# Full 128-row key and query blocks in the attentions of a two-layer encoder

## The chip, the cores and the metric

One core of one Trainium2 chip runs the whole program. The metric is device time in microseconds of one execution, as the median of several runs.

## The reference

Two pre-norm residual layers work on 1040 tokens: 16 learned meta tokens ahead of 1024 real ones, 1024 features wide, in float32.

```
layer 0:  oa = diff_attention(qa, ka, va)     4 heads, two softmaxes each, relative bias
          ob = gqa_dense(qb, kb, vb)          8 query heads on 2 key heads, normed and rotated
          h += concat(oa, ob) @ w_out
layer 1:  oc = window_gqa(qc, kc, vc)         16 query heads on 2 key heads, |i-j| <= 128,
          h += oc @ w_out                     the 16 meta keys always seen, a sink per head
both:     h += relu(norm(h) @ w_up)**2 @ w_down
out = norm(h)[16:]
```

In `diff_attention` the weights are `softmax(q0 k0) - lam * softmax(q1 k1)`, over all 1040 keys. In layer 1 only the 1024 real queries are needed, since the meta rows are dropped at the end.

## The kernel before, in words

Activations lie transposed, features on partitions and tokens along columns. A float32 product is done as several float32r passes over high and low parts (`kh`, `kl`, `vh`, `vl`, `ph`, `plo`), each part exact.

Tokens are cut in tiles of 128, with a ninth tile of 16: 1040 = 8 x 128 + 16. In layer 0 the tokens lie with the meta tokens first, so the ninth tile holds the last 16 tokens, as queries and as keys.

*Layer 0, projections.* `natural` (L292 to 300) transposes values to [token, feature], four tiles to a PSUM bank, the ninth as 16 rows; `store_v` and `load_v` pass them through DRAM, the ninth tile with a DMA of its own.

*Layer 0, attention.* `head_a` handles a differential head in four groups of query tiles, (0, 1), (2, 3), (6, 7, 8), (4, 5); `attend_b` handles two query tiles of a grouped-query head, 16 pairs for each key head, and one further group per key head with the 16 queries of the ninth tile of four heads side by side (64 rows). For a query tile `scores` makes q k in three chunks of 346 or 348 keys in PSUM, VectorE moves them to SBUF with the row minimum (L504, L507), and ScalarE takes the exponential (L516). A differential tile is then combined on POOL (L619, L620). The ninth query tile of a differential head has its two softmaxes in rows 0 to 15 and 32 to 47 of one 48-row tile; a matmul with `sel48` transposes and sums them (L545).

`pv` (L523 to 574) then multiplies with the values. The keys are taken in runs of two blocks for a 256-column group (one for the 272-column group (6, 7, 8)): transpositions to PSUM (`tr`, L543), a copy to `ph` on ScalarE (L557), the low part `plo` by a subtraction on VectorE (L559), and value matmuls to `pv` (L572). The ninth block is a run of its own:

```
kw = TW[runs[r][0]]
...
T.matmul(ps_o[:, :gw], vmats[v][:kw, j, :], (plo if lo else ph)[:kw, c],
         start=n_ == 0, stop=n_ == total - 1)
```

with `kw` = 16: two value matmuls over 16 rows for a grouped-query group (`passes` are (values, ph) and (values, plo)), three for a differential one (a third with the values' low part).

*Layer 1, attention.* For 8 pairs of heads and 8 query tiles (L1163 to 1248), scores cover two or three key blocks and the 16 meta keys, which lie between the blocks along the columns of the keys (400 or 272 columns). The values are multiplied by pairs of items; the meta keys are the last item, and their value matmuls go over `kw` = 16 rows (L1233). Their transposition takes 128 columns of the scores, and so brings 112 rows of other keys along; only in the last query tile (t = 7) the meta keys end the columns, and 16 are transposed.

*Order.* Code is written in dependency order, and a scheduler puts each engine's instructions in an order of its own ahead of time. Attention work is offered to it in pieces: `late` holds the value products of up to three groups (two in layer 1), whose pieces are run between scores. Each engine then runs its queue in order.

Of the kernel before, what the change touches and what calls it, by code (L numbers as in the profile page):

```python
# [74 lines left out]
def trunk(tc, hT, gT, w_in0, w_out0, w_up, w_down, w_in1, w_out1, rel, sinks, lamv, subln, qkn,  # L75
# [13 lines left out]
    def lay_out(pl, tags):  # L89
        """fix where a pool's slots lie: a first tile of each tag, in this order, handed to its first users."""  # L90
# [47 lines left out]
    def load_w(src, lo_on=V, parts=1, to=None):  # L138
        """a [128, 8 x 128] tile of weights as the split halves of its columns."""
# [6 lines left out]
    def mm3(ps, w, xh, xl, o, n, k0=0, k1=KT):  # L146
        """ps[:, :n] = the product over k from k0 to k1 (added to what is there if k0 > 0), columns o to o + n."""
# [6 lines left out]
    def rsqrt_small(x, pw, n):  # L154
        """1/sqrt(x) of a [pw, n] tile by three Newton steps from the shifted-exponent guess."""
# [27 lines left out]
    def colsum(acc, c0, n, ps, scale, eps=None):  # L183
        """rows of mean(acc over partitions)+eps, one column for each token tile, then 1/sqrt."""
# [20 lines left out]
    def bcast_cols(y, tiles, newps, use):  # L205
        """use(psum, first column, width) gets y's entries laid along the free axis on every partition."""
# [58 lines left out]
    def project0(m, scale=None, w=None, raw=False, tags=()):  # L265
        """[128 columns of the projection, tokens] of the normed input; raw: without the norm's factor yet."""
# [15 lines left out]
    def spill_pair(i, parts):  # L282
        """high and low parts of [128, tokens] to DRAM; parts: [(source, first column, width)]."""
# [18 lines left out]
    def store_v(dst, v):  # L302
        D.dma_start(dst[:, :8 * P], f32(v[:, :8]).rearrange("p a b -> p (a b)"))
        D.dma_start(dst[:16, 8 * P:], f32(v[:16, 8]))

    def load_v(v, src):
        D.dma_start(f32(v[:, :8]).rearrange("p a b -> p (a b)"), src[:, :8 * P])
        D.dma_start(f32(v[:16, 8]), src[:16, 8 * P:])

    # axial rotary tables times the norm's gain  # L310
# [17 lines left out]
    def rope(z, tab, fscale, i_out):  # L328
        """normalize and rotate a pair of heads [2 x 64, tokens]."""
# [58 lines left out]
    natural(zv, put_v)  # L388
# [3 lines left out]
    # relative-position bias vectors, negated, to DRAM  # L392
# [5 lines left out]
    # each copied to 128 rows: read back with a row pitch shorter by one, row p is shifted by p  # L398
# [19 lines left out]
    # lambda  # L418
# [10 lines left out]
    lam48 = cst.tile([48, 1], F32, name="lam48")  # L429
    V.memset(lam48, 1.0)  # L430
    V.tensor_copy(lam48[32:48], nlam[32:48])
    sel48 = cst.tile([48, 16], F32, name="sel48")
    V.memset(sel48, 0.0)
    for r in (0, 32):
        D.dma_start(sel48[r:r + 16], ident_d[0:16, 0:16])
# [7 lines left out]
    for h in range(4):  # L443
# [9 lines left out]
        natural(project0(8 + h), put)  # L453
        store_v(vA_d[h, 0], vh)
        store_v(vA_d[h, 1], vl)
# [236 lines left out]
    for g in range(2):  # L692
# [8 lines left out]
        for i in range(4):  # L701
            for t in range(0, 8, 2):
                if 4 * i + t // 2 == B_TAIL[g]:
                    attend_b(g, [(qt[:, :], 64)], store_t)
# [653 lines left out]
```

## Time and profile before

| | |
|---|---|
| median of 3 runs | 2626.34 us (2625.93 to 2629.81) |
| span of the profiled execution | 2630.9 us (the profile gives no further time of its own) |
| TensorE busy | 2508.9 us, 95% of the span |
| VectorE busy | 1937.8 us, 74% |
| ScalarE, POOL busy | 1265.7 and 1281.2 us |
| mean granted TensorE clock | 0.979 of full speed |
| layer 0 attention | about 269 to 727 us |
| layer 1 attention | about 1558 to 1842 us |

In a timeline each row is a run of like instructions: start, duration up to the end of the last, engine, line, operation, output and inputs, weights as rows x columns, the moving operand, and the count. `16*128` are weights of 16 rows and 128 columns. A matmul's printed duration holds its way through the array, so that successive ones overlap; the distance of starts tells what one takes of TensorE.

### The profile page before, as it was taken

What the parts mean: (1) busy time and instruction counts of PE and PEld (TensorE: products, weight loads), DVE (VectorE), ACT (ScalarE), POOL (GpSimd) and SP (SyncE); (2) the same over time, 40 slices, a digit from 0 to 9 for tenths busy, and PEclk for the clock granted to TensorE, in tenths of its full rate; (3) what the DMA queues carried; (4) which work ended last, traced back from release to release, by engine and by line L of the source; (5) the groups of instructions that cost most, each with busy time, mean ns of one, the idle gap of its engine ahead of it and who ended that gap; (6) DMA issues with size and microseconds to landing.
All of it is one profiled execution on the core that took longest, in us unless ns stands there. A gap on an engine that the chain in (4) does not pass through costs nothing. (4 is left out here: it accounts for less than half of the span.)

```text
span 2630.9 us, 42960 instructions
## 1 busy us (share of the span) xinstructions
PE 2508.9 (95%) x15440; PEld 2233.5 (85%) x15440; DVE 1937.8 (74%) x4057; ACT 1265.7 (48%) x2562; POOL 1281.2 (49%) x1214
## 2 busy tenths in 40 slices
PE   7999999999998999989999999999989999899997
PEld 7999888888898899988999988887868888676776
DVE  7834887798748566689898757777575656989975
ACT  3322656677634344453433547777344444443434
POOL 3300765333145223268877344556453223889854
PEclk9999999999998999999999999999989999999998
DMA  4378433200131532323232342232312332233322
GB/s 133 117 243 260 111 95 93 49 11 11 67 123 42 173 114 98 114 82 105 82 106 90 117 120 71 65 88 61 121 44 101 112 112 96 96 96 98 102 75 80
DMA packets 105494, 261.09 MB, mean 99 GB/s; under 512 B 16864, under 2 KB 48320, under 8 KB 104768
## 3 DMA queue, kind: packets, MB, share of 16 engines
q1 hardware_dynamic: 105280, 258.35, 30.9%
q8 instruction: 121, 1.98, 0.3%
q14 instruction: 93, 0.76, 0.1%
HBM read 191.40 MB, written 75.40 MB: 101 GB/s over the span
## 5 line engine op out<-in xcount | busy, mean ns | idle before, releaser
L854 PE MATMUL st<-h,wh 128*128 128x260 f32 (+1 forms) x2520 | 811.9, 326 | 45.3 <-DVE h L998 14.5
L854 PE MATMUL st<-l,wh 128*128 128x260 f32 (+1 forms) x2520 | 810.2, 324 | 6.6 <-DVE l L779 4.0
L854 PE MATMUL st<-h,wl 128*128 128x260 f32 (+1 forms) x2520 | 782.9, 325 | 14.8 <-DVE wl L135 8.8
L854 PEld LDWEIGHTS st<-h,wh 128*128 128x128 f32 x2520 | 480.3, 191 | 98.9 <-DVE h L998 19.9
L854 PEld LDWEIGHTS st<-h,wl 128*128 128x128 f32 x2520 | 474.4, 191 | 63.0 <-POOL wl L135 12.8
L854 PEld LDWEIGHTS st<-l,wh 128*128 128x128 f32 x2520 | 481.8, 191 | 45.0 <-DVE l L779 4.6
L134 ACT CAST wh<-wr 128x512 fp32r<-128x512 f32 x378 | 233.3, 619 | 408.7 <-PE st L854 228.7
L135 DVE TENSOR_TENSOR wl<-wr,wh 128x512 fp32r<-128x512 f32 x254 | 215.0, 848 | 178.9 <-ACT wh L134 178.3
L864 POOL TENSOR_TENSOR ws<-wr 128x512 f32<-128x512 f32 x32 | 43.2, 1350 | 412.7 <-DMA wr<-w_up 332.1
L135 POOL TENSOR_TENSOR wl<-wr,wh 128x512 fp32r<-128x512 f32 x124 | 177.0, 1430 | 67.0 <-ACT wh L134 62.2
L502 PE MATMUL sc<-stk,stk 128*128 128x346 f32 (+1 forms) x768 | 186.4, 356 | 8.1 <-DVE mx L504 7.9
L886 ACT ACTIVATE up<-up 128x260 f32<-128x260 f32 (+1 forms) x192 | 93.7, 491 | 193.2 <-DVE up L885 193.1
L516 ACT ACTIVATE sp<-sp,mn 128x1040 f32<-128x1040 f32 (+1 forms) x134 | 156.2, 1166 | 38.6 <-DVE mn L514 37.0
L998 DVE TENSOR_TENSOR h<-h,st 128x260 f32<-128x260 f32 x392 | 151.7, 417 | 29.7 <-PE st L854 27.3
L559 DVE TENSOR_TENSOR plo<-tr,ph 128x512 fp32r<-128x512 f32 (+3 forms) x260 | 153.4, 598 | 24.1 <-ACT ph L557 23.2
L557 ACT CAST ph<-tr 128x512 fp32r<-128x512 f32 (+3 forms) x260 | 130.3, 515 | 82.1 <-PE tr L543 56.5
L572 PE MATMUL pv<-ph,v 128*128 128x256 f32 (+3 forms) x594 | 157.3, 302 | 0.8 <-ACT ph L557 0.7
L998 DVE TENSOR_TENSOR hall<-hall,st 128x512 f32<-128x512 f32 x196 | 131.9, 681 | 31.2 <-PE st L854 28.7
L151 PE MATMUL mm<-l,wh 128*128 128x346 f32 (+3 forms) x440 | 150.9, 344 | 1.3 <-DVE l L762 1.2
L151 PE MATMUL mm<-h,wl 128*128 128x346 f32 (+3 forms) x440 | 150.1, 343 | 0.0
L151 PE MATMUL mm<-h,wh 128*128 128x346 f32 (+3 forms) x440 | 148.5, 344 | 1.2 <-ACT h L761 1.2
L673 POOL TENSOR_SCALAR sp<-sp,rsum 128x1040 f32<-128x1040 f32 (+1 forms) x66 | 74.2, 1138 | 152.5 <-DVE rsum L520 123.0
(273 smaller groups left out, 5943.0 us busy)
## 6 DMA issues: line engine op xcount, KB each, us to landing
wr<-w_down SPq DMA_DIRECT2D x68, 512.0 KB, 3.6
wr<-w_up SPq DMA_DIRECT2D x64, 512.0 KB, 3.5
stk<-stk_d SPq DMA_DIRECT2D x72, 260.0 KB, 7.0
sd<-up SPq DMA_DIRECT2D x28, 520.0 KB, 3.1
s<-sd SPq DMA_DIRECT2D x28, 520.0 KB, 3.1
sd<-up SPq DMA_DIRECT2D x28, 512.0 KB, 2.6
s<-sd SPq DMA_DIRECT2D x28, 512.0 KB, 3.5
wr<-w_in SPq DMA_DIRECT2D x27, 512.0 KB, 3.8
```

The lines of the kernel that those rows point to most:

```text
L134: A.copy(h, src)
L135: lo_on.tensor_tensor(l, src, f32(h), op=ALU.subtract)
L151: T.matmul(ps[:, :n], a[:, k % 4 * P:(k % 4 + 1) * P], x[k][:, o:o + n], start=(k == 0 and i == 0), stop=(k == len(xh) - 1 and i == 2))
L502: T.matmul(ps[:M, :n], q, k[:, o:o + n], start=(i == 0), stop=(i == len(ops) - 1))
L516: A.activation(s[:M, :L], s[:M, :L], AF.Exp, bias=mn[:M, x:x + 1], scale=-1.0, accum_out=sums[:M, x:x + 1])
L557: A.copy(ph[:kw, :w], pt[:kw, :w])
L559: V.tensor_tensor(plo[:kw, :w], pt[:kw, :w], f32(ph[:kw, :w]), op=ALU.subtract)
L572: T.matmul(ps_o[:, :gw], vmats[v][:kw, j, :], (plo if lo else ph)[:kw, c], start=n_ == 0, stop=n_ == total - 1)
L673: G.tensor_scalar(s[:M], s[:M], rs[:M, i:i + 1], 1.0, op0=ALU.mult, op1=ALU.mult)
L854: T.matmul(acc_[x, o][:, :n], a[:, c], b[:, o:o + n], start=first and k == 0 and y == 0, stop=k == nk - 1 and y == 2, skip_group_check=not ...
L886: A.activation(r[:, c], r[:, c], AF.Square)
L998: marks[0].append(V.tensor_tensor(ht[m][:, c], ht[m][:, c], acc_[x, o][:, :n], op=ALU.add).ins)
```

## The change

All value and selector matmuls of both attentions come to use 128 rows.

*Layer 0 keys.* `pv` takes eight whole blocks. For the last 16 keys it transposes the last 128 columns (keys 912 to 1039) and copies rows 96 to 127, whose lower half are the 16 keys, once for each pass into rows 0 to 31, 32 to 63 and 64 to 95 of a `tail` tile that was zeroed at the start; the low part is subtracted in place. One matmul multiplies it with a block of values that stacks the same tail: `natural_tail` writes the 16 value columns into columns 16 to 31 of each 32 of a padded tile (`vtail`), transposes that, and the third copy becomes the low part. So the two or three 16-row matmuls of a group become one.

*Layer 0 queries.* `qt` of a differential head and its selector are 128 wide, and the meta group of a grouped-query head is 128 wide (64 of them zero).

*Layer 1.* The value blocks become ten: eight of keys, one with the 16 meta values in rows 0 to 15 and zeros below, one with them in rows 112 to 127 and zeros above (for t = 7, where the last 128 columns are transposed). The meta item's copies and matmuls go over 128 rows; their number is as before.

The value tile is stored and loaded with one DMA; 646 instructions stand in the queue of SP in place of 663.

```diff
-    def natural(z, use):
-        for b in range(0, NT, 4):
-            n = min(4, NT - b)
+    vtail = pP.tile([P, 4, 32], F32, tag="vtail", bufs=1, name="vtail")
+    G.memset(vtail, 0.0)
+    def natural_tail(z, n, use):
+        A.copy(vtail[:, 0:n, 16:32], z[:, S:L].unsqueeze(1).to_broadcast([P, n, 16]))
+        pt = bank("nat")
+        T.transpose(pt[:, 0:P], vtail.rearrange("p a b -> p (a b)"), ident)
+        use(pt, 8, 1, P)
+    def natural(z, use, nt=NT):
+        for b in range(0, nt, 4):
+            n = min(4, nt - b)
...
-        natural(project0(8 + h), put)
+        def put_tail(pt, b, n, w):
+            A.copy(vh[:, 8], pt[:, :P])
+            V.tensor_tensor(vh[64:96, 8], pt[64:96, :P], f32(vh[64:96, 8]), op=ALU.subtract)
+        zv = project0(8 + h)
+        natural(zv, put, 8)
+        natural_tail(zv, 3, put_tail)
...
+    tails = [pA.tile([P, 272], F32R, tag="tail", bufs=3, name=nm("tail")) for _ in range(3)]
+    for t in tails:
+        G.memset(f32(t), 0.0)
...
-                    T.matmul(ps_o[:, :gw], vmats[v][:kw, j, :], (plo if lo else ph)[:kw, c],
-                             start=n_ == 0, stop=n_ == total - 1)
+                    T.matmul(ps_o[:, :gw], vmats[v][:, j, :], (plo if lo else ph)[:, c],
+                             start=n_ == 0, stop=False)
                     n_ += 1
+        yield
+        pt, _ = transposed([L - P])
+        tl = tails[tail_at[0] % 3]
+        tail_at[0] += 1
+        for x, (v, lo) in enumerate(passes):
+            rows = slice(32 * x, 32 * x + 32)
+            if lo:
+                V.tensor_tensor(tl[rows, :gw], pt[96:128, :gw], f32(tl[0:32, :gw]), op=ALU.subtract)
+            else:
+                A.copy(tl[rows, :gw], pt[96:128, :gw])
+        T.matmul(ps_o[:, :gw], vmats[0][:, 8, :], tl[:, :gw], start=False, stop=True)
...
-        qt = pA.tile([P, 2, 48], F32R, tag="qt", name=nm("qt"))
+        qt = pA.tile([P, 2, P], F32R, tag="qt", name=nm("qt"))
...
-        qt = pA.tile([P, 64], F32R, tag="qtb", bufs=2, name=nm("qt"))
+        qt = pA.tile([P, P], F32R, tag="qtb", bufs=2, name=nm("qt"))
+        G.memset(f32(qt[:, 64:P]), 0.0)
...
-                items = [(b, o, P) for b, o in blocks] + [(8, mo, NM)]
+                items = blocks + ((8, mo) if t < 7 else (9, wd - P),)
...
-                            T.matmul(po[:, :256], vp[g][:kw, b, :], pp[:kw, 256 * x:256 * x + 256], start=first,
+                            T.matmul(po[:, :256], vp[g][:, b, :], pp[:, 256 * x:256 * x + 256], start=first,
                                      stop=last and y == 1)
```

The scheduler's order moves with it. On TensorE, in the middle of the grouped-query heads, before: the ninth block of one group (`pv_6159`) stands as two value matmuls on `ph_6215` and `plo_6217`, six rows apart, with scores (`sc`) and the next group's first value matmul (`pv_6265`) between them.

```order
L502 MATMUL sc_6441<-stk_5187,stk_5212 128x348 [waits DVE_49]
L502 MATMUL sc_6441<-stk_5193,stk_5212 128x348
L572 MATMUL pv_6159<-ph_6215,v_5199 128x256 [waits Activation_49]
L502 MATMUL sc_6445<-stk_5187,stk_5212 128x346 [waits DVE_49]
L502 MATMUL sc_6445<-stk_5193,stk_5212 128x346
L572 MATMUL pv_6265<-ph_6271,v_5199 128x256 [waits Activation_49]
L502 MATMUL sc_6449<-stk_5187,stk_5212 128x346 [waits DVE_49]
L502 MATMUL sc_6449<-stk_5193,stk_5212 128x346
L572 MATMUL pv_6159<-plo_6217,v_5199 128x256 [waits DVE_49]
L543 MATMUL tr_6292<-ident,sp_5909 128x128 [waits PE_49]
```

The same place in the change: one matmul on a `tail` tile ends the group `pv_6198`, after the next group's scores and its first value matmul.

```order
L521 MATMUL sc_6471<-stk_5143,stk_5167 128x348 [waits DVE_49]
L521 MATMUL sc_6471<-stk_5149,stk_5167 128x348
L521 MATMUL sc_6475<-stk_5143,stk_5167 128x346 [waits DVE_49]
L521 MATMUL sc_6475<-stk_5149,stk_5167 128x346
L521 MATMUL sc_6479<-stk_5143,stk_5167 128x346 [waits DVE_49]
L521 MATMUL sc_6479<-stk_5149,stk_5167 128x346
L586 MATMUL pv_6301<-ph_6307,v_5155 128x256 [waits Activation_49]
L599 MATMUL pv_6198<-tail_2530,v_5155 128x256 [waits DVE_49]
L555 MATMUL tr_6328<-ident,sp_5954 128x128 [waits PE_49]
L555 MATMUL tr_6328<-ident,sp_5971 128x128
```

Two matmuls with a wait each became one with one; the transpositions that feed it (`tr_6251`) stand 22 rows ahead of it, and over all 50 tails 15 to 37 rows ahead. In layer 1 TensorE's order stays as it was, but for a few places late in it; in the dense layers it stays.

## Rows read from the trace of the kernel before

**Rows 1.** Busy us (and instructions) by window: PE, PEld, DVE, ACT, POOL, granted clock, DMA

```profile
269.00:465.00 196.00, 187.93 (x1226) 163.16 (x1225) 160.62 (x609) 122.83 (x241) 122.66 (x102) 0.97 0.38 98
500.00:690.00 190.00, 189.28 (x1357) 169.92 (x1355) 168.97 (x583) 145.86 (x279) 61.90 (x55) 1.00 0.08 24
...
1560.00:1780.00 220.00, 219.06 (x1279) 184.00 (x1277) 160.61 (x412) 162.49 (x419) 112.74 (x207) 1.00 0.27 73
```

**Rows 2.** Timeline of TensorE in the grouped-query heads: full matmuls and transpositions

```profile
590.77 0.28 PE L572 MATMUL pv<-plo,v 128*128 128x256 f32 x1
590.89 0.28 PE L572 MATMUL pv<-ph,v 128*128 128x256 f32 x1
...
592.24 0.60 PE L543 MATMUL tr<-ident,sp 128*128 128x128 f32 x4
592.60 0.36 PE L572 MATMUL pv<-plo,v 128*128 128x256 f32 x1
```

**Rows 3.** The same timeline around a value matmul over 16 rows

```profile
592.91 0.28 PE L572 MATMUL pv<-plo,v 128*128 128x256 f32 x1
593.12 0.38 PE L572 MATMUL pv<-ph,v 16*128 16x256 f32 x1
593.43 0.66 PE L543 MATMUL tr<-ident,sp 128*128 128x128 f32 x4
```

**Rows 4.** Timeline of TensorE in the windowed heads around a pair

```profile
1644.44 0.28 PE L1233 MATMUL pv<-plo,vp 128*128 128x256 f32 x1
1644.65 0.38 PE L1233 MATMUL pv<-ph,vp 16*128 16x256 f32 x1
1644.87 0.27 PE L1233 MATMUL pv<-plo,vp 16*128 16x256 f32 x1
1645.07 0.66 PE L1224 MATMUL tr<-ident,s 128*128 128x128 f32 x4
```

**Rows 5.** Timeline of TensorE in a differential head, one group's tail

```profile
469.80 0.39 PE L572 MATMUL pv<-ph,v 16*128 16x272 f32 x1
...
470.92 0.39 PE L572 MATMUL pv<-plo,v 16*128 16x272 f32 x1
471.15 0.28 PE L572 MATMUL pv<-ph,v 16*128 16x272 f32 x1
```

**Rows 6.** The same timeline around a selector pair of the meta queries

```profile
461.98 0.38 PE L543 MATMUL tr<-ident,sp 128*128 128x128 f32 x2
...
462.61 0.39 PE L572 MATMUL pv<-plo,v 128*128 128x272 f32 x1
```

**Rows 7.** Groups of TensorE by form, 264 to 727 us, and (last row) 1555 to 1845 us

```profile
L572 PE MATMUL pv<-ph,v 16*128 16x256 f32 x56 | 20.2, 360 | 0.0
L572 PE MATMUL pv<-plo,v 16*128 16x256 f32 x44 | 16.5, 376 | 0.0
L545 PE MATMUL tr<-sel,sp 48*128 48x16 f32 x64 | 12.5, 270 | 0.0
...
L1233 PE MATMUL pv<-ph,vp 16*128 16x256 f32 x64 | 24.4, 381 | 0.0
```

**Rows 8.** Groups of VectorE by form, 500 to 690 us: busy us, mean ns

```profile
L559 DVE TENSOR_TENSOR plo<-tr,ph 16x256 fp32r<-16x256 f32 x27 | 10.9, 404 | 0.0
```

**Rows 9.** Waits, 500 to 690 us: us in total, times, longest

```profile
ACT ph L557 <- PE tr L543: 31.0, 57, 2.7
...
DVE plo L559 <- ACT ph L557: 7.2, 19, 0.9
DVE rsum L520 <- ACT sp L516: 4.9, 11, 0.5
```

**Rows 10.** Busy us by window at a turn of differential heads

```profile
430.00:440.00 10.00, 7.75 (x55) 6.82 (x55) 9.75 (x34) 4.83 (x9) 7.41 (x7) 0.97 0.03 12
```

**Rows 11.** Groups of ScalarE by form, 255 to 727 us

```profile
L557 ACT CAST ph<-tr 16x256 fp32r<-16x256 f32 x44 | 15.6, 355 | 14.3 <-PE tr L543 12.8 <-DVE plo L559 0.7 <-DVE mx L504 0.7
```

**Rows 12.** Waits, 270 to 465 us

```profile
PEld pv L572 <- DVE plo L559: 4.7, 8, 2.3
```

More of the change, by code (lines that the diff above doesn't have):

```diff
@@ L428, in trunk @@
     V.tensor_scalar(nlam, nlam, -LAM_INIT, None, op0=ALU.add)
[L429 to L433, printed above, removed]
+    lam2 = cst.tile([P, 1], F32, name="lam2")
+    V.memset(lam2, 1.0)
+    V.tensor_copy(lam2[32:48], nlam[32:48])
+    sel2 = cst.tile([P, 16], F32, name="sel2")
+    V.memset(sel2, 0.0)
     for r in (0, 32):
-        D.dma_start(sel48[r:r + 16], ident_d[0:16, 0:16])
+        D.dma_start(sel2[r:r + 16], ident_d[0:16, 0:16])
     sln = cst.tile([P, 1], F32, name="sln")
@@ L523, in pv @@
     def pv(ps_o, ptiles, vmats, passes, lo_pool=()):
-        gw = sum(c for _, _, c, _ in ptiles)
+        gw = sum(c for _, c, _ in ptiles)
         nb = max(1, 512 // gw)
-        runs = []
-        for b in range(0, NT, nb):
-            blocks = list(range(b, min(b + nb, NT)))
-            if len(blocks) > 1 and TW[blocks[-1]] < P:
-                runs += [blocks[:-1], blocks[-1:]]
-            else:
-                runs.append(blocks)
-        def split(r):
-            run = runs[r]
-            kw = TW[run[0]]
-            pt = bank("tr")
-            for i, j in enumerate(run):
-                off = i * gw
-                for p, r_, cw, sel in ptiles:
-                    if sel is None:
-                        T.transpose(pt[:kw, off:off + cw], p[:r_, j * P:j * P + kw], ident[:r_, :r_])
-                    else:
-                        T.matmul(pt[:kw, off:off + cw], p[:r_, j * P:j * P + kw], sel, start=True, stop=True)
-                    off += cw
-            w = len(run) * gw
+        runs = [list(range(b, min(b + nb, 8))) for b in range(0, 8, nb)]
@@ new lines, in transposed @@
+        def transposed(blocks):
+            pt = bank("tr")
+            off = 0
+            for o in blocks:
+                for p, cw, sel in ptiles:
+                    if sel is None:
+                        T.transpose(pt[:, off:off + cw], p[:, o:o + P], ident)
+                    else:
+                        T.matmul(pt[:, off:off + cw], p[:, o:o + P], sel, start=True, stop=True)
+                    off += cw
+            return pt, off
+        def split(r):
+            pt, w = transposed([j * P for j in runs[r]])
@@ L563, in pv @@
         order = [r for r in range(len(runs)) if r not in slow] + list(lo_pool)
-        n_, total = 0, NT * len(passes)
+        n_ = 0
         for r in order:
@@ L567, in pv @@
             ph, plo = slow[r] if r in slow else split(r)
-            kw = TW[runs[r][0]]
             for i, j in enumerate(runs[r]):
@@ L677, in values @@
             yield from pv(po, ptiles, (vp[g],), ((0, 0), (0, 1)), LO_B)
-            gw = sum(c for _, _, c, _ in ptiles)
+            gw = sum(c for _, c, _ in ptiles)
             t = getA("ob", [64, 256], F32, 2)
@@ L1142, in trunk @@
     zv = project_kv(9)
-    vp = [pC.tile([P, NT, P], F32R, tag="v", bufs=2, name=nm("vp")) for _ in range(2)]
-    for b in range(0, NT, 4):
-        n = min(4, NT - b)
-        w = P if b < 8 else NM
+    vp = [pC.tile([P, 10, P], F32R, tag="v", bufs=2, name=nm("vp")) for _ in range(2)]
+    zm = pC.tile([P, 2, P], F32, tag="zm", bufs=1, name="zm")
+    G.memset(zm, 0.0)
+    A.copy(zm[:, 0, 0:NM], zv[:, 0:NM])
+    A.copy(zm[:, 1, P - NM:P], zv[:, 0:NM])
+    for b in range(0, 10, 4):
+        n = min(4, 10 - b)
         pt = bank("tr")
         for i in range(n):
-            o = 16 + (b + i) * P if b < 8 else 0
-            T.transpose(pt[:w, i * P:(i + 1) * P], zv[:, o:o + w], ident)
-        src = pt[:w, :n * P].rearrange("p (a b) -> p a b", b=P)
+            o = 16 + (b + i) * P
+            T.transpose(pt[:, i * P:(i + 1) * P], zv[:, o:o + P] if b < 8 else zm[:, i], ident)
+        src = pt[:, :n * P].rearrange("p (a b) -> p a b", b=P)
         for g in range(2):
             sg = src[:, :, 64 * g:64 * g + 64]
-            A.copy(vp[g][:w, b:b + n, 0:64], sg)
-            V.tensor_tensor(vp[g][:w, b:b + n, 64:128], sg, f32(vp[g][:w, b:b + n, 0:64]), op=ALU.subtract)
+            A.copy(vp[g][:, b:b + n, 0:64], sg)
+            V.tensor_tensor(vp[g][:, b:b + n, 64:128], sg, f32(vp[g][:, b:b + n, 0:64]), op=ALU.subtract)
     def kcol(b):
```

80 lines of the change are left out of this document (37 added, 43 removed).

## The prediction, made before the changed kernel ran

> **What bounds the kernel now.** Three views were read in this order: busy time in windows cut at the stages, the start times of the matmuls inside them, and the waits.
>
> The windows [rows 1] show the three stretches that the change touches. In the differential attention (269 to 465 us) TensorE is busy 187.93 of 196 us and VectorE 160.62. In the grouped-query attention (500 to 690) it is 189.28 of 190, with VectorE at 168.97 and ScalarE at 145.86. In the windowed attention (1560 to 1780) it is 219.06 of 220, with the other two at 161 and 162. So TensorE paces all three; VectorE is close behind it in the second, and the third has room everywhere else. Projections and dense layers outside these stretches keep their work.
>
> A busy TensorE says nothing of how well the time is used, because the printed durations of matmuls overlap. The start times do. Two value matmuls with full 128 x 128 weights and 256 columns start at 590.77 and 590.89, 0.12 us apart [rows 2]. A value matmul over the last 16 keys breaks that rhythm: the one before it starts at 592.91, it starts at 593.12, and the next transposition only at 593.43 [rows 3]. That is 0.52 us, of which 0.12 belongs to the first: a lone 16-row matmul costs **0.40 us**, over three times a full one. In the windowed attention two stand together: 1644.44, 1644.65, 1644.87, then the transposition at 1645.07 [rows 4]. Less 0.12 this is **0.51 us for a pair**, and even between the two, with nothing switched, 0.22 us pass. In the differential attention a group has one lone (469.80) and one pair (470.92 and 471.15) [rows 5].
>
> The 48-row selector matmuls of the meta queries show it too: two transpositions and two selectors take 461.98 to 462.61 = 0.63 us [rows 6], while four transpositions take 592.24 to 592.60 = 0.36 us [rows 2].
>
> **What the change saves on TensorE.** By the loops there are 16 x 3 + 32 x 2 = 112 value matmuls over 16 rows in the 48 full groups of layer 0; the groups by form show 56 + 44 of them with 256 columns, the other 12 lie in the four wider groups. They show 64 selectors in 32 pairs, and in the windowed attention 64 such matmuls of high parts, with as many of low parts [rows 7].
>
> *Grouped-query heads*, 32 groups of two, which stand alone as in rows 3: 2 x 0.40. In their place comes one full matmul over the stacked block, 0.12. That is 0.68 us a group, 21.8 us.
>
> *Differential heads*, 16 groups: 0.40 + 0.51 - 0.12 = 0.79 each, 12.6 us. The 32 selector pairs: a selector over 128 rows with 16 columns is not in the trace. I price it as a transposition, which has the same 128 x 128 weights; a pair then saves 0.63 - 0.36 = 0.27 us, 8.6 us in all (bounds: nothing, and 0.63 less the 0.18 of two transpositions, 0.45 a pair).
>
> *Windowed heads*, 64 pairs: the count stays, each matmul becomes full. 0.51 - 0.24 = 0.27 us a pair is 17.3 us; a pair that other work tears apart saves 0.80 - 0.24 = 0.56, and all torn would be 35.8. The rows show it together, so I stay near that end: 20 us.
>
> Sum on TensorE: 21.8 + 21.2 + 20 = 63 us.
>
> Here a rule of the Trainium skill speaks against the change: "TensorE: Matmul & The Clock Gate", section "Why this matters for your kernels", has a single matmul with 32 rows take the same time as one with 128, and finds the gain of small row counts in running several at once. The rows above do not agree, 0.22 us against 0.12 [rows 2, 4]; what the rule would leave of the gain is the third rival.
>
> **How much of it reaches the end.** *Windowed heads:* with both other engines near 73% nothing else takes over. 19 of 20 us, a little off for the waits at its two ends.
>
> *Grouped-query heads:* the window from 500 to 690 us holds 27 tails [rows 8], so TensorE asks for 27 x 0.68 = 18.4 us less, 172 us. VectorE needs 169 us for the same work, since the tail's subtraction keeps its 256 columns (0.404 us). VectorE also waits 7.2 us on ScalarE's copies and 4.9 us on its exponentials [rows 9]. If both waits stay, the window ends at 169 + 12 = 181 us; if both vanish, at TensorE's 172. ScalarE's copies themselves wait 31.0 us on transpositions [rows 9], which will come sooner, so I take 179: 11 us. The other 5 groups lie in stretches that mix with other stages; I count 2 of their 3.4 us. **13 us.** VectorE is what is late next here.
>
> *Differential heads:* VectorE has 35 us of slack in 196. But at the turn of heads it leads already: from 430 to 440 us it is busy 9.75 of 10, and TensorE 7.75 [rows 10]. About a fifth of each head is of that kind, and gains nothing: **17 us** of 21.2.
>
> *What is added:* three memsets of 272 columns ahead of POOL's first work, and in the windowed set-up one more transposition and two small copies: together some 0.5 us. Five copies of the value tail into the padded tile, each ahead of a transposition, at most the 0.355 us of a 16 x 256 copy [rows 11]: 1 us. The two meta groups of the grouped-query heads now have 128 columns, so one round of 512 columns becomes two, at twice the 0.404 us of 256 columns on VectorE [rows 8]: 1.6 us. Together **3 us**. The differential tails need 16 more ScalarE copies of 0.355 us; ScalarE works 122.83 of 196 us there [rows 1], which hides their 5.7 us; without that cover they would cost that much. The 17 fewer DMAs are taken at nothing: none of the waits above is theirs. The meta queries' score matmuls keep their columns with more rows of output, and are taken at nothing: TensorE and VectorE go by columns in the rows above (16 x 256 takes 0.404 us on VectorE, and TensorE's 0.12 us is for full tiles).
>
> Sum: 19 + 13 + 17 - 3 = **46 us**. The profile gives the profiled execution's span alone, 2630.9 us, which lies 4.6 us above the median of the runs. 46 us off the span is 2585; off the median it is 2626.3 - 46 = **2580 us**.
>
> **The rivals.**
>
> *VectorE takes over early.* In layer 0 it is the near second, and 179 us assumes that it is busy 94% of the window, against 89% now. For it: its waits on ScalarE, which the change does not touch. Against it: 9.75 of 10 us in one window [rows 10]. At 91% the grouped-query window ends at 185 us and gains 5; I halve the differential heads to 8 and leave the windowed ones 17. 5 + 8 + 17 - 3 = 27 us, 2599 us.
>
> *All of it comes.* The waits shrink as TensorE runs ahead: 63 - 3 = 60 us, 2566 us.
>
> *Rows cost nothing.* If a 16-row matmul took what a full one takes, and the gaps had another cause (a wait for the tail's copies), only the 112 - 48 = 64 dropped matmuls would be saved, 64 x 0.12 = 7.7 us, less 3: 2622 us. Against it: the transposition behind a 16-row matmul, which needs nothing of the tail, also starts late, 0.31 and 0.20 us after it [rows 3, 4]. This is the rival that the skill's rule above would have.
>
> *Slower: TensorE stands at the tail.* The stacked block needs a copy, a subtraction and, in the differential heads, a second copy before its one matmul. TensorE runs in order, so all later score and value matmuls would queue behind it, and VectorE and ScalarE behind those. The longest wait of a value matmul for such a subtraction in the differential stretch is 2.3 us [rows 12]. The gain is gone where the 50 tails wait 46 / 50 = 0.9 us each; at 1.5 us it would be 75 - 46 = 29 us slower, 2655 us. Against it: the new order keeps 15 to 37 instructions between the tail's transpositions and its matmul, 1.8 us or more at 0.12 each, while the chain takes 0.355 + 0.404 + 0.355 = 1.1 us.
>
> A lower granted clock is not priced: from 430 to 440 us it was still 0.97, with TensorE busy 7.75 of 10 [rows 10], and a stretch that VectorE paces would leave TensorE busier than that.
>
> **How the numbers follow.** Forecast 0.57, VectorE early 0.22, all of it 0.14, rows cost nothing 0.03, slower 0.04. The range goes from 2558 (all of it, and half of the torn pairs' further 16 us) to 2605 (VectorE early, with the additions at twice their 3 us and as much again of new stalls). A measurement of this kernel tells about 0.2%, 5.3 us, from no change: faster 0.57 + 0.22 + 0.14 = 0.93; within it 0.03, the rival with rows free; slower 0.04.
>
> **What would show it.** Value matmuls with 128 rows alone, with starts 0.12 us apart through the tail; the work of today's 1560 to 1780 us shorter by about 19; VectorE above 93% in the grouped-query stretch, with TensorE waiting for it there; 16-column selectors about 0.11 us apart. The prediction is wrong if a tail still takes 0.4 us or more from TensorE, if TensorE stands before the tail matmul, or if the grouped-query stretch does not shorten.

## The result, and the profile after

The changed kernel takes **2586.18 us** (median of 4 runs, 2583.45 to 2588.05) beside 2628.07 us before (4 runs, 2625.93 to 2630.96): a ratio of 0.9827, interval 0.9807 to 0.9847 (the quotient of the two medians, 0.984, lies in it), some 42 to 45 us. 2580 was forecast, and 2558 to 2605 as the range. The profiled execution took 2583.45 us.

The head of the page of the changed kernel: the span, then the busy time of each engine, its share of the span and its instructions.

```profile
span 2581.6 us, 42774 instructions
...
PE 2450.0 (95%) x15375; PEld 2221.3 (86%) x15375; DVE 1945.1 (75%) x4059; ACT 1278.5 (50%) x2587; POOL 1287.9 (50%) x1221
```

TensorE is still busy 95% of the span. As in the prediction, it is the starts of matmuls that tell what became faster. The timeline of TensorE in the grouped-query heads of the changed kernel, around the stacked tail (start, duration, line, operation):

```profile
580.33 0.28 PE L586 MATMUL pv<-ph,v 128*128 128x256 f32 x1
580.45 0.28 PE L599 MATMUL pv<-tail,v 128*128 128x256 f32 x1
580.57 0.60 PE L555 MATMUL tr<-ident,sp 128*128 128x128 f32 x4
```

The tail takes 0.12 us like any other, and what follows starts at once; a lone 16-row matmul took 0.40 [rows 3]. The same view at a selector pair of the meta queries:

```profile
458.56 0.38 PE L555 MATMUL tr<-ident,sp 128*128 128x128 f32 x2
458.78 0.29 PE L557 MATMUL tr<-sel,sp 128*128 128x16 f32 x2
458.92 0.37 PE L586 MATMUL pv<-ph,v 128*128 128x272 f32 x1
```

Two transpositions and two selectors take 0.36 us, where it was 0.63 [rows 6]. In the windowed heads, the meta keys' pair can no longer be told from the matmuls ahead of it [rows 4]:

```profile
1576.49 0.28 PE L1256 MATMUL pv<-plo,vp 128*128 128x256 f32 x1
1576.61 0.28 PE L1256 MATMUL pv<-ph,vp 128*128 128x256 f32 x1
...
1576.95 0.28 PE L1256 MATMUL pv<-plo,vp 128*128 128x256 f32 x1
1577.07 0.71 PE L1249 MATMUL tr<-ident,s 128*128 128x128 f32 x5
```

**Where the time came from.** Each trace is cut at the same six places of TensorE's work (first transposition of the attention, last transposition for the differential norms, last value matmul of layer 0, first projection matmul of the windowed heads, their last value matmul, last dense matmul). Lengths in us; "again" is the control run of the first experiment.

| stretch | before | after | again |
|---|---|---|---|
| ahead of the attention | 269.4 | 268.8 | 268.2 |
| differential heads | 229.5 | 218.2 | 219.4 |
| grouped-query heads | 226.2 | 206.9 | 207.0 |
| dense part of layer 0 | 799.3 | 798.8 | 800.2 |
| windowed heads | 317.8 | 305.8 | 304.9 |
| dense part of layer 1 | 726.6 | 720.8 | 721.6 |
| rest | 62.1 | 62.4 | 62.2 |

So 11, 19 and 12 us in the three attentions, and 6 us where the change touches nothing. One trace tells a stretch to a few us only: the two profiled executions lie 49 us apart, the medians 42. In those traced kernels below that keep the changed kernel's code in a stretch, the differential heads took 217.5 to 221.5 us, the grouped-query heads 206.8 to 208.5, the windowed heads 303.4 to 305.8.

The second cut is by cause: for each matmul, what its step to the next start exceeds the undisturbed step of its form in the same trace (0.12 us for 256 columns, 0.36 for four transpositions). The excess is summed in three lots: steps into or out of fewer than 128 rows; steps at the half clock; the rest, which are waits and small gaps.

| stretch, kernel | few rows | waits, gaps | half clock |
|---|---|---|---|
| differential, before | 20.0 | 27.7 | 10.3 |
| differential, after | 0.6 | 32.3 | 15.0 |
| grouped-query, before | 19.2 | 21.7 | 0.0 |
| grouped-query, after | 0.0 | 27.5 | 0.0 |
| windowed, before | 23.7 | 27.7 | 5.0 |
| windowed, after | 0.3 | 39.1 | 5.0 |

62.0 us of few-row steps are gone (19.4 + 19.2 + 23.4), and 64 dropped matmuls of 0.12 add 7.7. Of these 70 us some 26 came back: 21.8 as waits (4.6 + 5.8 + 11.4), 4.7 as half clock. How the waits divide hangs on what is taken as undisturbed: with the median step of each form, the waits grow by 7.8, 4.5 and 7.8 us, and with the half clock it is 26 again. So the total is firmer than its parts, which are sure to some 4 us.

What the waits are is read from the windows and the waits of the changed kernel. The windows (busy us and instructions of PE, PEld, DVE, ACT, POOL, then granted clock), in the order of the program:

```profile
268.00:455.00 187.00, 174.60 (x1206) 162.64 (x1206) 167.78 (x635) 132.36 (x264) 126.93 (x104) 0.95 0.43 112
...
490.00:660.00 170.00, 167.79 (x1286) 160.84 (x1284) 166.47 (x570) 144.48 (x271) 59.58 (x53) 1.00 0.06 15
1528.00:1730.00 202.00, 198.31 (x1238) 176.23 (x1237) 154.14 (x399) 157.27 (x407) 108.28 (x197) 1.00 0.26 66
```

In the grouped-query heads VectorE is now busy 166.47 of 170 us, 98%, from 89% [rows 1], and TensorE's weight loads wait for its low parts (6.7 us; in the kernel before no such wait is listed from 500 to 690 us). The waits of the changed kernel, 490 to 690 us (us in total, times, longest):

```profile
ACT ph L572 <- PE tr L555: 12.1, 20, 1.2
...
ACT tail L598 <- PE tr L555: 7.2, 12, 3.0
...
PEld pv L586 <- DVE plo L574: 6.7, 21, 0.4
DVE plo L574 <- ACT ph L572: 4.2, 8, 1.0
...
DVE tail L596 <- ACT tail L598: 0.9, 1, 0.9
```

Rows 9 count the tails with the blocks. ScalarE's wait for transpositions so fell from 31.0 us to 19.3 (12.1 + 7.2), VectorE's wait for ScalarE's copies from 7.2 to 5.1 (4.2 + 0.9), and its wait for the exponentials, 4.9, is no longer listed. In the differential heads TensorE waits at the scores: of its waits, 268 to 490 us,

```profile
PEld sc L521 <- DVE mx L523: 16.0, 24, 2.2
...
PE sc L521 <- DVE mx L523: 9.9, 13, 1.9
```

and of those of the kernel before, in the same 222 us:

```profile
PEld sc L502 <- DVE mx L504: 7.5, 11, 2.5
...
PE sc L502 <- DVE mx L504: 4.8, 4, 2.3
```

In the windowed heads VectorE and ScalarE are busy only 76 and 78%, and still TensorE stops. Its longest waits in these heads, before (1524.4 to 1842.3 us) and after (1492.6 to 1798.5):

```profile
PE tr L1224 <- POOL s L1207: 2.6, 2, 2.4
PE sc L1196 <- DVE mx L1198: 2.3, 4, 1.0
...
PE pv L1233 <- DVE plo L1229: 0.2, 1, 0.2
```

```profile
PE tr L1249 <- POOL s L1235: 4.4, 3, 2.7
PE sc L1224 <- DVE mx L1226: 2.5, 4, 1.2
PE pv L1256 <- DVE plo L1252: 2.0, 3, 0.9
PE pv L1256 <- ACT ph L1251: 1.3, 3, 0.6
```

All listed waits of its matmuls there are 6.3 us before and 12.2 after: more for the probabilities that POOL scales, and now for high and low parts too. The timeline of all engines at one of them:

```profile
1581.07 1.29 POOL L135 TENSOR_TENSOR wl<-wr,wh 128x512 fp32r<-128x512 f32 x1
...
1581.18 1.72 DVE L1120 TENSOR_TENSOR q<-zq,q 64x512 fp32r<-64x512 f32 x1
...
1582.93 0.69 DVE L1252 TENSOR_TENSOR plo<-tr,ph 128x512 fp32r<-128x512 f32 x1
...
1583.68 0.39 PE L1256 MATMUL pv<-plo,vp 128*128 128x256 f32 x1 [0.89 <-DVE plo L1252]
```

A low part comes late because VectorE was splitting the next queries (1.72 us, beside a POOL subtraction; half of these take at most 0.687), and TensorE waits 0.89 us.

**The 6 us of the untouched stretch.** Half of them are the clock's. About 100 us into layer 1's dense part, while TensorE waits for a norm, the kernel before worked 10.2 us at half speed and this one 3.4. The same 32 us of work, in the kernel before and then after (columns as in the windows above):

```profile
1924.00:1956.00 32.00, 24.59 (x85) 19.46 (x86) 27.06 (x31) 13.48 (x23) 19.30 (x15) 0.73 0.10 34
```

```profile
1880.00:1912.00 32.00, 25.19 (x97) 19.88 (x98) 28.22 (x38) 14.81 (x25) 19.38 (x15) 0.84 0.10 33
```

A granted clock of 0.73 against 0.84, and 85 matmuls against 97. Followed matmul by matmul (both kernels have the same 3215 here), the lead grows by 2.8 us at this place. Of all kernels traced, three had 10.2 us at half speed here: the one before, and the two below whose windowed heads or layer 0 are as before. Ten had 3.4 and one none. The instructions are the same; why the clock came back sooner no run shows. The other 3 us of lead come later and were not taken apart. Over all kernels traced, none of which touches this stretch, it took 720.8 to 727.3 us, so no run shows these 6 us to be the change's.

### The profile page after: what moved, and what is told of

Same layout as the page of the kernel before. It is cut to its first block, busy times and chain, and to the rows that moved or that the text cites. A ratio compares the mean times of both kernels' runs of the same rounds, so it can differ in the third digit from the quotient of the medians.

```text
span 2581.6 us, 42774 instructions
## 1 busy us (share of the span) xinstructions
PE 2450.0 (95%) x15375; PEld 2221.3 (86%) x15375; DVE 1945.1 (75%) x4059; ACT 1278.5 (50%) x2587; POOL 1287.9 (50%) x1221
## 5 line engine op out<-in xcount | busy, mean ns | idle before, releaser
L535 ACT ACTIVATE sp<-sp,mn 128x1040 f32<-128x1040 f32 x134 | 156.4, 1168 | 41.9 <-DVE mn L533 37.3
L135 DVE TENSOR_TENSOR wl<-ws,wh 128x512 fp32r<-128x512 f32 x120 | 129.2, 1077 | 24.0 <-ACT wh L134 23.7
L696 POOL TENSOR_SCALAR sp<-sp,rsum 128x1040 f32<-128x1040 f32 x66 | 75.3, 1153 | 143.0 <-DVE rsum L539 61.0
L151 PE MATMUL proj<-hg0l,wh 128*128 128x346 f32 (+1 forms) x416 | 137.1, 330 | 9.3 <-DVE hg0l L245 9.3
L574 DVE TENSOR_TENSOR plo<-tr,ph 128x512 fp32r<-128x512 f32 (+1 forms) x212 | 135.9, 646 | 11.4 <-ACT ph L572 10.1
```

The costliest lines, as they stand in the source:

```text
L135: lo_on.tensor_tensor(l, src, f32(h), op=ALU.subtract)
L151: T.matmul(ps[:, :n], a[:, k % 4 * P:(k % 4 + 1) * P], x[k][:, o:o + n], start=(k == 0 and i == 0), stop=(k == len(xh) - 1 and i == 2))
L535: A.activation(s[:M, :L], s[:M, :L], AF.Exp, bias=mn[:M, x:x + 1], scale=-1.0, accum_out=sums[:M, x:x + 1])
L574: V.tensor_tensor(plo[:, :w], pt[:, :w], f32(ph[:, :w]), op=ALU.subtract)
L696: G.tensor_scalar(s, s, rs[:, i:i + 1], 1.0, op0=ALU.mult, op1=ALU.mult)
```

## The experiments

**The change again, on one chip with three others.** No edit.

> The changed kernel once more, beside the three below on one chip, as their reference. If the first result was no accident of its executions, the ratio to the kernel before is again between 0.981 and 0.985. In its profile the dense stretch of layer 1 tells whether the 5.8 us that it seemed to gain belong to the change: no instruction moved there, so I expect 721 to 727 us, whatever the half-speed clock of that execution makes of it, and the same in the kernels beside it.

2587.3 us (5 runs, 2583.51 to 2589.41), ratio 0.9832 (0.9816 to 0.9847): the first result stands. The dense part of layer 1 took 721.6 us.

**Is it the number of rows?** The layer-1 part alone, on the kernel before:

```diff
-    vp = [pC.tile([P, NT, P], F32R, tag="v", ...
+    vp = [pC.tile([P, 10, P], F32R, tag="v", ...
...
-                items = [(b, o, P) for b, o in blocks] + [(8, mo, NM)]
+                items = blocks + ((8, mo) if t < 7 else (9, wd - P),)
```

> The kernel before with the layer 1 part of the change alone. Rows theory (a matmul over 16 rows holds TensorE longer than one over 128, and that is where the time came from): between the first key projection of layer 1 and its last value matmul the changed kernel gained 12 us, so 12 us here, about 2616 us, ratio 0.9955. Number rival (the gain is the dropped matmuls and their waits): layer 1 drops none, so 0 us, ratio 1.000.

2619.95 us, ratio 0.9948 (0.993 to 0.9967). The windowed heads took 304.0 us, 13.8 less than before, the rest as before; few rows 0.3 us, waits 34.9. Then, in the changed kernel, the meta keys' value matmuls back to 16 rows, with the padded data and the same number of instructions:

```diff
+                            kw = NM if b == 8 else P
-                            T.matmul(po[:, :256], vp[g][:, b, :], pp[:, 256 * x:256 * x + 256], start=first,
+                            T.matmul(po[:, :256], vp[g][:kw, b, :], pp[:kw, 256 * x:256 * x + 256], start=first,
```

> The changed kernel with the value matmuls of the meta keys in layer 1 over 16 rows again, for query tiles 0 to 6; the number of instructions, the copies and the layout are those of the change. Rows theory: 7 eighths of layer 1's gain is lost, some 10 us, about 2596 us, and layer 1 takes as long as before. Number rival: no difference, 2586 us.

2597.85 us, ratio 0.9866 (0.9844 to 0.9888). The windowed heads took 317.4 us, as before the change. The timeline of TensorE in this run:

```profile
1586.17 0.28 PE L1257 MATMUL pv<-plo,vp 128*128 128x256 f32 x1
1586.38 0.38 PE L1257 MATMUL pv<-ph,vp 16*128 16x256 f32 x1
1586.69 0.66 PE L1249 MATMUL tr<-ident,s 128*128 128x128 f32 x4
```

From the full matmul to the transposition 0.52 us, to the hundredth what rows 3 show. Instruction for instruction the same work, only fewer rows, and TensorE's order in these heads is that of the change up to the 1576th of 1818 matmuls: rows alone cost it. The third run asks whether 64 rows do so too, in the stacked tail of the grouped-query heads:

```diff
-        T.matmul(ps_o[:, :gw], vmats[0][:, 8, :], tl[:, :gw], start=False, stop=True)
+        k = 32 * len(passes) if len(passes) == 2 else P
+        T.matmul(ps_o[:, :gw], vmats[0][:k, 8, :], tl[:k, :gw], start=False, stop=True)
```

> The changed kernel, with the 32 stacked tail matmuls of the grouped-query heads over the 64 rows that hold anything instead of 128; same instructions, same data, the rest full. If any change in the number of rows costs TensorE, as rows 3 show it for 16 rows, 32 x 0.28 = 9 us come back on TensorE and the stretch of these heads gets 5 to 9 us longer. Rival: what costs is the very small tile (16 or 32 rows), and 64 rows run like 128: no difference, the stretch stays at 207 us and a 64-row tail starts 0.12 us after the matmul before it.

2589.34 us, ratio 0.9839 (0.9824 to 0.9853); the grouped-query heads took 209.7 us, 2.8 more. TensorE's timeline in this run:

```profile
599.82 0.60 PE L555 MATMUL tr<-ident,sp 128*128 128x128 f32 x4
600.35 0.38 PE L600 MATMUL pv<-tail,v 64*128 64x256 f32 x1
600.67 0.66 PE L555 MATMUL tr<-ident,sp 128*128 128x128 f32 x4
```

The tail starts 0.53 us after four transpositions that take 0.36, and the next waits 0.32 us for it. The few-row lot is 9.9 us, as theory asked (32 x 0.28 = 9), with TensorE's order in this stretch unchanged; but the waits fell from 27.5 to 20.6, so that only 2.8 us reached the end (1.2 to 2.9 beside the 206.8 to 208.5 of the other traces). The rows theory is right for 64 rows as for 16, and the 5 to 9 us expected were wrong: in this stretch TensorE's own time is worth less than a third of itself.

**The differential heads in parts.** The meta queries back to 48 rows:

```diff
-                        T.matmul(pt[:, off:off + cw], p[:, o:o + P], sel, start=True, stop=True)
+                        T.matmul(pt[:, off:off + cw], p[:48, o:o + P], sel[:48], start=True, stop=True)
...
-        qt = pA.tile([P, 2, P], F32R, tag="qt", name=nm("qt"))
+        qt = pA.tile([P, 2, 48], F32R, tag="qt", name=nm("qt"))
```

> The changed kernel with the differential heads' meta query tile, its softmax and its selector back at 48 rows; everything else full. Rows theory: 32 selector pairs at 0.27 us ask TensorE for 8.6 us more; the differential heads turned about 4 tenths of what TensorE saved into time, so 3 to 4 us slower than the change, about 2590 us. Number rival: as many instructions, so the change's time, 2586 us.

2594.86 us, ratio 0.9853 (0.9833 to 0.9874); the differential heads 226.1 us. More than twice what was expected. So the other part was taken back instead, with the meta tile full:

```diff
-                yield from pv(po, ptiles, (vh, vl), ((0, 0), (0, 1), (1, 0)), LO_A)
+                yield from pv16(po, ptiles, (vh, vl), ((0, 0), (0, 1), (1, 0)), LO_A)
```

where `pv16` is the value function of the kernel before.

> The changed kernel, with the values of the differential heads over the last 16 keys as before (three matmuls over 16 rows, two transposed tiles of 16 columns), the full meta query tile kept. With the run that put the meta queries back at 48 rows, it splits the 11 us of these heads. If the two parts act each by itself, this one loses what that one left: about 3.5 us, to 222 us for the differential heads. If TensorE asks for 12.6 us less and VectorE lets only part of the sum through, either part alone is worth more than its share of the sum: 6 to 9 us lost, to 224 to 227.

2599.13 us, ratio 0.9878 (0.9862 to 0.9893); 226.0 us. And both taken back:

> The changed kernel with all of the differential heads as before: three matmuls over the last 16 keys and meta queries of 48 rows; the grouped-query and the windowed heads stay changed. Each part alone left these heads at 226 us, both together at 218 to 219. If the parts support each other (with one kind of short tile left, what the other frees goes back into waits, and only when both are gone does it come), this one is where the kernel before is, 229 us, and its time is 10 to 12 us over the changed kernel's 2587: the parts are worth 3 each by themselves and 11 together. If instead each part is worth 7 to 8 and the kernel before happened to have a lucky order here, it comes to 233 or more. The grouped-query heads stay at 207, the windowed heads at 305.

2603.0 us, ratio 0.9867 (0.9846 to 0.9888). The profiled execution was the longest of the four, 2611.73 us, and its differential heads took 236.7 us with 31 us at half clock; up to the third norm they ran as in the kernel before (176.7 us after the start, then 176.0). The lots of the four cases:

| differential heads | length | few rows | waits, gaps | half clock |
|---|---|---|---|---|
| as before | 229.5 | 20.0 | 27.7 | 10.3 |
| values full | 226.1 | 10.3 | 34.5 | 11.1 |
| meta full | 226.0 | 10.2 | 36.1 | 6.9 |
| both | 218.2 | 0.6 | 32.3 | 15.0 |

Either part alone takes 10 us of few-row steps away and gets 7 to 8 back as waits; the second takes 10 more, and the waits do not rise again. By the ratios either part alone is worth nothing sure (0.9853 and 0.9878 against 0.9867), both together 0.9867 - 0.9832 = 0.0035, 9 us. The run with meta queries of 48 rows holds the order still: in these heads VectorE, ScalarE and POOL run the changed kernel's sequence, and TensorE's differs in 6 of 1399 places. So rows alone cost here too: 226.1 us, beside 217.5 to 221.5 in the seven traces with the change's heads, means that 5 to 9 of the 9.7 us of few-row steps reach the end. The run with the values as before has 24 matmuls more and another order. What the waits do over the four cases therefore mixes rows with order, and why they go up first and then down stays open.

**What paces the grouped-query heads?** If VectorE at 98%, relieving it must help. The output additions to a ScalarE copy and a POOL addition:

```diff
-OC_B, OC_C = 0, 5
+OC_B, OC_C = 1, 5
```

> The changed kernel with the output additions of the grouped-query heads moved from VectorE (0.40 us each, 34 of them) to a ScalarE copy and a POOL addition. If VectorE paces that stretch now (98% busy): up to 34 x 0.32 = 11 us off VectorE, 5 to 9 us faster than the change, 2577 to 2581 us, with TensorE busier again. If TensorE or ScalarE paces it: no gain, or slower, since ScalarE is at 85% and gets 34 x 0.37 = 12.6 us more.

2594.56 us, ratio 0.9858 (0.9837 to 0.9879): the opposite. The grouped-query heads took 212.4 us. The windows of this run, in the middle of the stretch:

```profile
520.00:660.00 140.00, 137.81 (x1034) 129.99 (x1034) 129.19 (x437) 121.99 (x243) 65.97 (x68) 1.00 0.05 11
```

and of the changed kernel:

```profile
520.00:660.00 140.00, 138.21 (x1057) 132.14 (x1056) 137.38 (x471) 120.00 (x225) 50.61 (x45) 1.00 0.06 16
```

VectorE fell to 92%, and TensorE got through 1034 matmuls instead of 1057. VectorE waits for ScalarE instead; of this run's waits, 500 to 660 us:

```profile
DVE plo L574 <- ACT ph L572: 8.7, 21, 1.5
PEld pv L586 <- DVE plo L574: 7.4, 23, 0.5
```

and of the changed kernel's, in the same window:

```profile
PEld pv L586 <- DVE plo L574: 5.5, 17, 0.4
...
DVE plo L574 <- ACT ph L572: 0.4, 2, 0.2
```

As I read it, a copy of 0.37 us on ScalarE delays the high part behind it, and that delays VectorE. The second try gave ScalarE nothing more:

```diff
-LO_A = ()
-LO_B = ()
+LO_A = (0,)
+LO_B = (0,)
```

> The changed kernel, with the first 512 columns of each group of layer 0 (both kinds of heads) split by POOL: ScalarE copies them out of PSUM as it did, POOL makes the high and the low part, and VectorE is rid of one subtraction of 0.68 us in each of 50 groups, some 23 us in the grouped-query heads. The run that gave ScalarE and POOL the output additions lost time although VectorE was relieved, so two theories stand. If VectorE is the pace of the grouped-query heads, this one, which gives ScalarE nothing more, makes them 4 to 8 us shorter than 207 us, since 27.5 us of TensorE's time there are waits and gaps against 21.7 before the change. Rival: the pace is the path of a block through ScalarE and the engine that subtracts, whichever it is; POOL needs about 2.5 us for its two steps, TensorE waits for it instead, and the stretch is as long or longer (207 to 214). For the differential heads the same: 2 to 5 us shorter, or none.

The third gave the blocks more buffers:

```diff
-C_S, C_PH = 5, 3
+C_S, C_PH = 5, 4
...
-    getA = lay_out(pA, [("sp", [P, L], F32, A_SP), ("osq", [P, L], F32, 1), ("ph", [P, 512], F32R, 3),
-                        ("plo", [P, 512], F32R, 3), ...
+    getA = lay_out(pA, [("sp", [P, L], F32, A_SP), ("osq", [P, L], F32, 1), ("ph", [P, 512], F32R, 4),
+                        ("plo", [P, 512], F32R, 4), ...
```

> The changed kernel, with four buffers instead of three for the high parts and four for the low parts, in all three attentions. If TensorE's waits for low parts are the time that a block needs on its way through ScalarE and VectorE, one more block under way hides part of them: 2 to 4 us less in the grouped-query heads (207) and in the windowed heads (305). If an engine's throughput is the pace, as VectorE's 9.8 of every 10 us say for the grouped-query heads, a buffer gives nothing there; and if in the windowed heads the waits are bursts of work on two engines, nothing there either: within 1 us in all three.

2609.98 us, ratio 0.9927 (0.9913 to 0.9941), and 2597.38 us, ratio 0.9875 (0.9859 to 0.9891): both lose, and both first of all at a place that neither theory named. The timeline of the run with four buffers, at the end of layer 0's attention:

```profile
682.97 0.38 PE L599 MATMUL pv<-tail,v 128*128 128x256 f32 x1
...
684.77 4.77 SPq L778 DMA_DIRECT2D l<-mixd  x8
...
689.88 2.10 PE L151 MATMUL mm<-h,wh 128*128 128x348 f32 x6 [6.53 <-ACT h L785]
```

TensorE stands for 6.5 us, since the loads of the next stage start 1.8 us after the last value matmul. In the changed kernel they start 37.4 us ahead of it, and 82 projection matmuls run between the last heads; here none do, nor in the run with low parts by POOL. In both, layer 0's attention holds two more tiles of 512 columns, 4 KB of each partition. As I read it the next stage's loads wait for that space; no run took space alone.

In the stretch itself the four buffers change nothing: 1285 matmuls from 490 to 660 us, against 1286. So one more block under way hides nothing there, as it should be where an engine's throughput is the pace. The windowed heads took 305.8 us and the differential heads 219.6, as in the change. In the run with low parts by POOL, VectorE is down to 147.49 of 170 us in the same window, and TensorE gets only 1213 matmuls done:

```profile
490.00:660.00 170.00, 163.34 (x1213) 151.97 (x1212) 147.49 (x517) 133.97 (x256) 106.55 (x103) 1.00 0.04 11
```

TensorE's matmuls there wait 5.9 us for high parts (490 to 690 us), in the changed kernel 0.7. So VectorE is full in the change, but both ways to empty it lengthened another wait; its 98% are the pace only in the sense that TensorE's savings stop there (the 64-row run), not that any relief pays. The differential heads, where VectorE is less full, came out at 215.8 us in the POOL run, 2 to 4 less than in the change and its control, and 1.7 below the lowest trace with the change's heads.

**The windowed heads.** The query splits to POOL:

```diff
-        V.tensor_tensor(q0[64:128], src[0:64], f32(q0[0:64]), op=ALU.subtract)
-        V.tensor_tensor(q1[0:64], src[64:128], f32(q1[64:128]), op=ALU.subtract)
+        G.tensor_tensor(q0[64:128], src[0:64], f32(q0[0:64]), op=ALU.subtract)
+        G.tensor_tensor(q1[0:64], src[64:128], f32(q1[64:128]), op=ALU.subtract)
```

> The changed kernel, with the two subtractions that split the queries of the windowed heads (twice for each pair of heads, 0.686 us each, 32 in all) on POOL instead of VectorE. Theory: the windowed heads gained 12 instead of 19 us because ScalarE and VectorE are full around these splits (5.8 to 5.9 of 6 us from 1578 to 1584 and 1596 to 1602) and TensorE waits there for the low parts; without 1.4 us of VectorE's work at each, the 270 us of these heads get 2 to 5 us shorter. Rival: POOL, which needs twice as long for a subtraction, hands the queries over later and the score matmuls wait for them: no gain or a few us longer. Second rival: the wait is ScalarE's, nothing changes.

2588.35 us, ratio 0.9826 (0.9806 to 0.9847), the control beside it 0.9832: no difference that the time shows. The profiled execution was the fastest, 2577.82 us, with 301.0 us for these heads; that is 3.9 less than the control's 304.9, and its half-clock lot is 4.1 less (3.2 against 7.3), while its waits are 35.4 us against 35.8. Of TensorE's own waits in these heads, those for low parts fell from 2.4 to 0.3 us and those for POOL went, while those for the scores' buffers and for high parts rose from 3.4 to 6.4. The traced execution lies 10 us below the other three, so its trace tells little of them. Then, besides, the additions from ScalarE and POOL to VectorE:

```diff
-OC_B, OC_C = 0, 5
+OC_B, OC_C = 0, 1
```

> The run with the query splits on POOL, and besides the output additions of the windowed heads by VectorE for seven of eight query tiles instead of three: ScalarE loses 32 copies of 0.37 us, POOL 32 additions of 0.74 us, VectorE gains 32 additions of 0.42 us. The query splits alone took 19 of VectorE's 154 us and gave nothing that the time shows. If the waits in the windowed heads come from several engines being full for a few microseconds at each split, with ScalarE the fullest left (159 of 202 us), these heads get 2 to 4 us shorter than 301 to 305. Rival: TensorE's waits there depend on the order in which a tile's steps stand in the queues, and not on how full an engine is: within 2 us.

2584.5 us (4 runs, 2583.64 to 2586.08), ratio 0.9804 (0.9788 to 0.9819), beside a kernel before of 2636.68. These heads took 302.3 us, 2.6 less than the control at the same clock there (10 us at half speed in both). ScalarE is busy 151.92 of the 202 us, from 156.74, and VectorE 138.57, from 153.93. The windows of the control and of this run:

```profile
1528.00:1730.00 202.00, 197.34 (x1232) 175.32 (x1231) 153.93 (x398) 156.74 (x404) 107.55 (x196) 1.00 0.25 64
```

```profile
1528.00:1730.00 202.00, 198.44 (x1243) 177.01 (x1242) 138.57 (x397) 151.92 (x385) 120.36 (x201) 1.00 0.25 65
```

It is the lowest ratio measured, but its interval touches the control's: a version a little better than the change, by 2.6 us in the trace (1.1 below the lowest of the unchanged windowed heads), not surely in the time.

## Why the prediction was right, and where its terms were not

**The mechanism** holds: few-row matmuls cost TensorE by their rows and not by their data. Putting 16 rows back, with the order of TensorE's work nearly unmoved, took away the 12 us that the windowed heads had gained, and 48 rows in the meta queries cost 5 to 9 us with it unmoved. "Rows cost nothing" falls. The rule of the Trainium skill behind that rival ("TensorE: Matmul & The Clock Gate", section "Why this matters for your kernels") does not hold for these matmuls among full ones: 0.40 us for one of 16 rows and 0.12 for a full one. Another page of the Trainium skill, "TensorEngine Tiling (Array Packing)", section "Tiling Modes", has a change of the tiling mode drain TensorE. The trace fits it, since the transposition behind a short matmul starts late too (0.31 us [rows 3], and 0.32 in the 64-row run); that these matmuls change the mode, and that it is a drain, no run here shows.

**TensorE's saving**, 63 us by the prediction, was 70: 19.2 + 3.8 = 23.0 in the grouped-query heads (21.8 forecast), 19.4 + 3.8 = 23.2 in the differential heads (21.2), 23.4 in the windowed heads (20). The selector price, made by analogy with a transposition, came out in the sum, 0.36 us for a pair and two transpositions (the median of 33), but not in its sign: the two selectors start 0.03 us apart and not 0.11.

**The share that reaches the end** was mis-sized in all three places. That the total came within 6 us of 2580 is luck in part, since the errors nearly cancelled:

- *Windowed heads: 19 forecast, 12 to 14 measured.* The step that failed is "with both other engines near 73% nothing else takes over". 11.4 us came back as waits (8.1 in the control). The average hid stretches of a few microseconds in which ScalarE and VectorE are full: both are busy 5.7 to 5.9 of 6 us from 1578 to 1584 and from 1596 to 1602. That the splits of queries make these waits was argued from one timeline, and taking the splits off VectorE gave nothing sure; less work for both engines gave 2.6 us, hardly beyond the spread of the traces. What makes the waits stays open.
- *Grouped-query heads: 13 forecast, 19 measured.* I let VectorE be busy 94% of the window and it was 98: ScalarE's wait for transpositions fell from 31.0 to 19.3 us, and of the 12.1 us that VectorE waited for ScalarE 5.1 were left. That VectorE is late next was right: the 64-row run took 9.9 us more of TensorE's time, and 2.8 showed.
- *Differential heads: 17 forecast, 11 measured*, and 10 in the control. I took a fifth off for the turns of heads. What came instead are 4.6 us of waits, most of the listed ones at the scores, and 4.7 of half clock (7 in the control): "a lower granted clock is not priced" was the other step that failed, since the granted clock fell from 0.97 [rows 1] to 0.95. That the change brings the half clock isn't sure: three traces with these heads as before have 17 to 31 us at half speed there, the seven with the change's heads 24 to 38.
- *What is added: 3 us.* The stretch ahead of the attention, with the padding of values, did not grow (269.4, then 268.8); the rest can't be seen apart. The traces have 20 DMA issues fewer on SP (744, then 724) where 17 were counted; both were taken at nothing.
- *The dense part of layer 1*, taken at nothing, gave 5 to 6 us, half of them by its clock; no run shows them to be the change's.

The three attentions gave 11.3 + 19.3 + 12.0 = 42.6 us, where 49 less 3 for what is added were forecast. "VectorE takes over early" was wrong in the grouped-query heads, its main place, and half right elsewhere. "TensorE stands at the tail" did not come: from 490 to 690 us no wait of a tail matmul is listed.

## What to carry to other kernels

Pad or stack a remainder of few rows among full matmuls into a full block, even where zeros do the work: here a lone matmul of 16 rows cost 0.40 us, one of 64 about as much, and a full one 0.12. Count what it frees on TensorE from the starts of matmuls, then ask in each stage what fills next, and look at windows of a few microseconds, not at the stage's mean. Before another engine is relieved, look at what the replacement puts ahead of the wait, and whether its buffers take the space that the next stage's loads need.

## What was not expected of the hardware

- A matmul of 64 rows breaks the rhythm as one of 16 does: with the transposition behind it 0.49 us (0.53 - 0.36 + 0.32), of which 0.12 is a full one's.
- The same subtraction on VectorE (64 x 512, L1120) took 0.687 us or less in half of its 16 executions and 1.72 at the longest, beside POOL's subtraction of 1.29 us; the one on the line above (L1119) took up to 2.37. The nine of both lines with no POOL instruction beside them took at most 0.687. Which of POOL's instructions do this was not tried.
- The half clock after the same break lasted 10.2 us in three kernels, 3.4 in ten and nothing in one, with the same instructions there. Between the kernel before and the changed one that moved 2.8 us.
